# Expert counts read twelve at a time, and the scatter planes paired, read back in 2 KB pieces and transposed later

## The chip, the cores and the metric

The kernel runs on one core of one Trainium2 chip. The metric is the device time of one execution in microseconds (us): the median of several runs.

## What is computed

The reference is a two-layer backbone over 256 context and 256 latent tokens of width 1024. Layer 0 mixes by gated linear attention beside grouped-query attention, layer 1 by a state-space scan beside a Fourier mixing. Every layer ends in a mixture of experts, which is where the change lies. Cut to that part:

```
idx, gates = route(tokens, router_w, router_b)      # top 2 of 16 experts for each token
y = moe_ffn(tokens, idx, gates, w_gate, w_up, w_down)   # sum over a token's two experts of
                                                    # gate * (silu(t @ w_gate) * (t @ w_up)) @ w_down
x = layer_norm(alpha * x + m_lat[5] * y[...])       # and the same for the context in layer 0
```

There are 16 experts with an inner width of 768. Layer 0 routes 512 tokens (context and latent), layer 1 routes the 256 latent ones.

## The kernel before, in words

**The expert loop.** `experts` (L1474) runs once for each layer. It walks over 16 experts `e`, two of which form a pair `p`. The tokens of a pair are packed into two slot blocks S = 0 and S = 1 of 64 slots for each expert; parts of 32 tokens that hold nobody are skipped at run time. For each expert `hidden` (L1654) multiplies the packed tokens by the gate and up weights and applies SwiGLU, and `down` (L1696) multiplies by the down weights one expert later. The weights of an expert are six transfers of 1.5 MB each (four for gate and up, two for down, L1646 to L1650), issued in a fixed order by SyncE (SP, `wload`, L334) into a ring of slots; a transfer waits until TensorE has finished with its slot.

**Counts.** `counts` (L1404) writes a table `cnt` of 25 integers: the tokens of each of 16 experts, the larger count of each of 8 pairs, and the largest of all. TensorE's sequencer reads one of them whenever `count` (L1736) is called: once for each expert, and twice for each pair but the first (once as `full`, once for `features`). Each read is a `value_load` with bounds, that is a register load, a register operation and an assertion. The branches of `when` (L1483, L1487) compare these registers with constants. The reads depend on nothing but the table, so the scheduler may issue them long before their use, and in bundles. GpSimd (POOL) reads pair counts of its own for `gather` (L1557) and `scatter` (L1602).

**Two ways back to the tokens.** In layer 0 the outputs of the first six pairs (NS = 6) go through DRAM. `scatter` (L1595) sends each pair's rows by indirect DMA into four DRAM tiles `plane0` to `plane3`, one for each quarter of 256 columns; a token has two rows there, one for each of its two experts. When pair 5 is scattered (at e = 12), `fetch(0)` (L1607) reads the 256 context tokens back with 16 DMAs of 128 KB on POOL's queue and adds the two rows on POOL; `collect` (L1619) transposes the sums on TensorE and adds them into the residual on VectorE (L1592). `collect(got, 0)` stands at the end of e = 13, where `fetch(1)` follows it into the same buffer, and `collect(got, 1)` at the end of e = 14. The remaining pairs, and all pairs of layer 1, go back by `combine` (L1629): VectorE builds eight one-hot matrices (L1588), in a buffer that shares its tag `rb` (one buffer) with that of `fetch`, and TensorE multiplies by them. `combine` of pair 6 runs in `between` (L1773) of e = 15.

**Order.** TensorE's matmuls in the loop are pinned to the order of the text (`self.pin`, L1760), except inside the branches of `when`. `between` runs after the first two parts of an expert's gate and up products, `middle` inside them. POOL's queue carries the scatters, the gathers of the next pairs' tokens (L1561) and the fetches, each in one order.

```
L1737  return nc.tensor.value_load(cnt[0:1, i:i + 1], min_val=0, max_val=T)
L1613  nc.gpsimd.dma_start(rb[:, j, i, q * 256:(q + 1) * 256], self.planes[q][o:o + 128])
L1801  if ns and 1 <= e - 2 * ns <= 2:
L1802      collect(got, e - 2 * ns - 1)
L1803      if e == 2 * ns + 1:
L1804          got = fetch(1)
```

## Time and profile before

| what | value |
|---|---|
| runs of the kernel before, us | 1477.24, 1477.56, 1483.76 (median 1477.56) |
| the profiled execution's own time, us | 1479.13 |
| its span in the profile, us | 1477.4 |
| mean granted TensorE clock, share of full speed | 0.921 |
| TensorE matmul busy (PE) | 1250.3 us, 85% |
| TensorE weight load (PEld) | 726.9 us, 49% |
| VectorE (DVE) | 682.2 us, 46% |
| ScalarE (ACT) | 398.0 us, 27% |
| GpSimd (POOL) | 140.8 us, 10% |
| transfers on SP's queue (q1) | 388.40 MB, 64.6% of 16 engines' span |
| transfers on POOL's queue (q0) | 17.71 MB, 3.3% |

The span is one execution from its first to its last instruction; the profiled execution's own time is a little longer than its span. Times in the rows are microseconds from the span's start, unless they are means or medians of one instruction, which are nanoseconds where the view says so. A timeline's row gives start, length, engine, line and operation, and in brackets how long the engine had been idle and what ended that; "issue" there means that the profile shows nothing it waited for. The letter q behind an engine (PEldq, SPq) stands for its sequencer.

### The profile page before, as it was taken

The numbers are of one execution on the slowest core, as the hardware profiler recorded it, in microseconds if no ns is written. First come the engines' busy times: TensorE is split into PE (matmuls) and PEld (weight loads), VectorE is DVE, ScalarE is ACT, GpSimd is POOL, SyncE is SP. The second block draws the span as 40 slices with busy tenths as digits, with TensorE's granted clock in tenths as the row PEclk, the third lists the DMA queues.
The fourth block names the chain that finished last, engine by engine and source line by source line (L and its number), as shares of the span: only waits on it lengthen the run. The fifth ranks groups of instructions, "written<-read, shape, count | busy, mean of one in ns | idle before, by whom it ended". The sixth has DMA issues, their size and how long they took to land. (4 is left out here: it accounts for less than half of the span.)

```text
span 1477.4 us, 27647 instructions
## 1 busy us (share of the span) xinstructions
PE 1250.3 (85%) x11433; PEld 726.9 (49%) x11434; DVE 682.2 (46%) x1773; ACT 398.0 (27%) x791; POOL 140.8 (10%) x153
## 2 busy tenths in 40 slices
PE   4999988898679799999878867998978688898774
PEld 0697553576334344554434435876833344454333
DVE  1847536876425111111123568737665245454445
ACT  2624234344110110111010134434431112121214
POOL 0000011102101111022133012002010000000000
PEclk8999999899799999999989988999989898998996
DMA  9421688134488998889998341273388999999981
GB/s 359 163 100 43 223 323 343 52 128 161 178 338 315 382 412 369 347 329 421 426 386 341 144 160 55 89 278 150 129 340 360 377 412 425 423 426 421 425 367 31
DMA packets 49475, 411.87 MB, mean 279 GB/s; under 512 B 7195, under 2 KB 11439, under 8 KB 18064
## 3 DMA queue, kind: packets, MB, share of 16 engines
q1 hardware_dynamic: 41200, 388.40, 64.6%
q0 software_dynamic: 7232, 17.71, 3.3%
q8 instruction: 140, 2.29, 0.6%
q10 hardware_dynamic: 864, 3.15, 0.5%
q14 instruction: 39, 0.32, 0.1%
HBM read 402.02 MB, written 13.11 MB: 281 GB/s over the span
## 5 line engine op out<-in xcount | busy, mean ns | idle before, releaser
L1665 DVE SCALAR_TENSOR_TENSOR h0p<-gu0p,gt0p,sg0p 128x192 f32<-128x192 f32 x64 | 25.3, 415 | 177.0 <-ACT sg0p L321 176.5
L345 PE MATMUL gu0p<-big,xe0p 128*32 128x384 f32 x992 | 91.8, 492 | 1.6 <-issue 1.4
L345 PE MATMUL gu1p<-more,big 128*32 128x384 f32 x976 | 85.5, 493 | 7.9 <-issue 3.0
L321 ACT ACTIVATE sg0p<-gu0p 128x192 f32<-128x192 f32 x64 | 19.6, 331 | 247.1 <-PE gu0p L345 243.8
L345 PE MATMUL gu0p<-ring,xe0p 128*32 128x384 f32 x768 | 74.8, 497 | 0.8 <-ACT sg0p L321 0.5
L345 PE MATMUL gu0p<-more,xe0p 128*32 128x384 f32 x800 | 74.7, 493 | 0.5 <-issue 0.5
L345 PE MATMUL ada<-ring,small 128*32 128x512 f32 x344 | 62.9, 684 | 14.2 <-DMA ring<-in_ada 14.2
L1665 DVE SCALAR_TENSOR_TENSOR h1p<-gu1p,gt1p,sg1p 128x192 f32<-128x192 f32 x48 | 19.9, 415 | 118.0 <-ACT sg1p L321 117.9
L345 PE MATMUL dp0p<-big,hT0p 128*32 128x256 f32 x792 | 59.4, 402 | 6.3 <-issue 4.0
L345 PEld LDWEIGHTS gu1p<-more,big 128*32 128x32 f32 x976 | 35.1, 111 | 51.3 <-issue 46.1
L345 PEld LDWEIGHTS gu0p<-big,xe0p 128*32 128x32 f32 x992 | 37.8, 111 | 45.4 <-issue 42.1
L321 ACT ACTIVATE y0p<-dp0p 64x512 f32<-64x512 f32 (+1 forms) x40 | 23.6, 591 | 132.9 <-PE dp0p L345 105.0
L321 ACT ACTIVATE y1p<-dp1p 64x512 fp32r<-64x512 f32 x64 | 37.9, 592 | 79.9 <-PE dp1p L345 79.1
L321 ACT ACTIVATE sg1p<-gu1p 128x192 f32<-128x192 f32 x48 | 15.9, 330 | 156.4 <-PE gu1p L345 141.0
L321 ACT ACTIVATE big<-big 128x512 f32<-128x512 f32 (+2 forms) x81 | 44.7, 575 | 48.8 <-DVE big L641 21.5
L1598 POOL DMA_INDIRECT plane<-y0p,to0p x36 | 35.6, 988 | 205.8 <-ACT y0p L321 180.0
L345 PE MATMUL zo<-zo,zw 128*128 128x256 f32 x384 | 54.7, 292 | 0.0
L345 PE MATMUL gu1p<-big 128*32 128x384 f32 x528 | 52.5, 510 | 0.0
L345 PE MATMUL dp0p<-ring,hT0p 128*32 128x256 f32 x624 | 48.9, 401 | 3.5 <-issue 3.2
L345 PEld LDWEIGHTS zo<-zo,zw 128*128 128x128 f32 x384 | 48.6, 191 | 6.6 <-issue 4.3
L345 PEld LDWEIGHTS <-zero 128*128 128x128 bf16 x105 | 10.0, 97 | 83.2 <-issue 64.8
L1730 DVE TENSOR_TENSOR y1p<-dp1p,y1p 64x512 fp32r<-64x512 f32 x64 | 44.0, 688 | 5.5 <-ACT y1p L321 3.9
(558 smaller groups left out, 2425.2 us busy)
## 6 DMA issues: line engine op xcount, KB each, us to landing
more<-in_egu SPq DMA_DIRECT2D x54, 1536.0 KB, 15.3
big<-in_egu SPq DMA_DIRECT2D x48, 1536.0 KB, 15.6
ring<-in_ada SPq DMA_DIRECT2D x27, 1536.0 KB, 8.0
ring<-in_ed SPq DMA_DIRECT2D x27, 1536.0 KB, 14.8
ring<-in_egu SPq DMA_DIRECT2D x26, 1536.0 KB, 13.5
big<-in_ed SPq DMA_DIRECT2D x21, 1536.0 KB, 12.9
more<-in_ed SPq DMA_DIRECT2D x16, 1536.0 KB, 10.7
ring<-in_odw SPq DMA_DIRECT2D x5, 1536.0 KB, 6.2
```

Of the source, the lines that this page charges most:

```text
L321: a = self.nc.scalar.activation(out, x, func, **kw)
L345: i = self.nc.tensor.matmul(out, lhsT, rhs, start=start, stop=stop, skip_group_check=True)
L1598: nc.gpsimd.indirect_dma_start(out=self.planes[q], out_offset=bass.IndirectOffsetOnAxis(ap=to[:, q, i, S:S + 1], axis=0), in_=Y[S][:, q // ...
L1665: nc.vector.scalar_tensor_tensor(H[:, t], p[:, 192:384], gt[:, 2 * m + t % 2, i, t // 2:t // 2 + 1], sg, op0=OP.mult, op1=OP.mult)
L1730: nc.vector.tensor_tensor(yl[r, q], dp[r], yh[r, q].bitcast(F32), op=OP.subtract)
```

## The change

Four things are changed, all in the expert stage.

1. The table of counts has the order first expert, second expert, larger of both, for each pair. TensorE reads it with one call for 12 entries (8 experts, 4 pairs) without assertions: at the start of the loop, and again at e = 6, queued behind the last matmul traced so far. `count` only looks the value up.
2. The four planes of 256 columns become two DRAM tiles, each with two quarters side by side (quarter `q` of a row is piece `2 * row + q % 2` of plane `q // 2`). The scatter's row numbers are doubled accordingly, and its four DMAs go out in the order 0, 2, 1, 3.
3. `fetch` reads with four DMAs of 512 KB, in pieces of 2 KB, instead of 16.
4. `collect(got, 1)` moves from the end of e = 14 to `between` of e = 15, ahead of `combine` of pair 6.

```
--- before.py
+++ after.py
@@ -343,6 +343,7 @@
 
     def mm(self, out, lhsT, rhs, start=True, stop=True):
         i = self.nc.tensor.matmul(out, lhsT, rhs, start=start, stop=stop, skip_group_check=True)
+        self.last = i.ins
         if self.pin:
             self.tc.keep_in_program_order(i)
 
@@ -450,11 +451,11 @@
 
     def open_planes(self, pool):
         nc = self.nc
-        z = pool.tile([128, 256], F32, name='zeros')
+        z = pool.tile([128, 512], F32, name='zeros')
         nc.gpsimd.memset(z, 0.0)
-        self.planes = [self.dram.tile([2 * T, 256], F32, name=f'plane{q}') for q in range(4)]
+        self.planes = [self.dram.tile([4 * T, 256], F32, name=f'plane{q}') for q in range(2)]
         for p in self.planes:
-            nc.gpsimd.dma_start(p.rearrange('(a p) d -> p a d', p=128), z.unsqueeze(1).broadcast_to([128, 8, 256]))
+            nc.gpsimd.dma_start(p.rearrange('(a p c) d -> p a (c d)', p=128, c=2), z.unsqueeze(1).broadcast_to([128, 8, 512]))
 
     def layer0(self):
         nc, tc = self.nc, self.tc
@@ -1404,17 +1405,18 @@
     def counts(self, l, count):
         nc, pm, rp = self.nc, self.pm, self.rp
         NP = NE // 2
-        cf = rp.tile([128, NE + NP + 1], F32, tag='r_cf', name=f'cf{l}')
-        nc.vector.tensor_copy(cf[:, :NE], count)
-        nc.vector.tensor_reduce(cf[:, NE:NE + NP], cf[:, :NE].rearrange('p (q m) -> p q m', m=2), axis=AX.X, op=OP.max)
-        nc.vector.tensor_reduce(cf[:, NE + NP:], cf[:, :NE], axis=AX.X, op=OP.max)
-        cnt = pm.tile([128, NE + NP + 1], I32, tag='r_cnt', name=f'cnt{l}')
+        cf = rp.tile([128, 3 * NP + 1], F32, tag='r_cf', name=f'cf{l}')
+        c3 = cf[:, :3 * NP].rearrange('p (q x) -> p q x', x=3)
+        nc.vector.tensor_copy(c3[:, :, 0:2], count.rearrange('p (q m) -> p q m', m=2))
+        nc.vector.tensor_reduce(c3[:, :, 2], c3[:, :, 0:2], axis=AX.X, op=OP.max)
+        nc.vector.tensor_reduce(cf[:, 3 * NP:], c3[:, :, 2], axis=AX.X, op=OP.max)
+        cnt = pm.tile([128, 3 * NP + 1], I32, tag='r_cnt', name=f'cnt{l}')
         nc.vector.tensor_copy(cnt, cf)
 
         wf = rp.tile([128, 2, NP], F32, tag='r_wf', name=f'wf{l}')
-        nc.vector.tensor_scalar(wf[:, 0], cf[:, NE:NE + NP], 0.0, None, op0=OP.is_gt)
+        nc.vector.tensor_scalar(wf[:, 0], c3[:, :, 2], 0.0, None, op0=OP.is_gt)
         for w in range(WIN[l], T >> l, WIN[l]):
-            nc.vector.tensor_scalar(wf[:, 1], cf[:, NE:NE + NP], float(w), None, op0=OP.is_gt)
+            nc.vector.tensor_scalar(wf[:, 1], c3[:, :, 2], float(w), None, op0=OP.is_gt)
             nc.vector.tensor_tensor(wf[:, 0], wf[:, 0], wf[:, 1], op=OP.add)
         nwin = pm.tile([128, NP, 2], I32, tag='r_nw', name=f'nwin{l}')
         nc.vector.tensor_copy(nwin, wf[:, 0].unsqueeze(2).broadcast_to([128, NP, 2]))
@@ -1483,13 +1485,13 @@
         def when(rv, least, yes, no=None):
             if rv is None:
                 return yes()
-            pin, self.pin = self.pin, False
+            pin, self.pin, last = self.pin, False, self.last
             with tc.If(rv > least) as cmp:
                 yes()
             if no:
                 with cmp.Else():
                     no()
-            self.pin = pin
+            self.pin, self.last = pin, last
 
 
 
@@ -1548,13 +1550,13 @@
                     if tail:
                         nc.vector.tensor_copy(tok[r, q], tg[s, 0, n - tail:])
                     if n > tail:
-                        nc.vector.tensor_copy(to[r, q], tg[s, 2])
+                        nc.vector.tensor_scalar(to[r, q], tg[s, 2], 2.0, q % 2 * 1.0, op0=OP.mult, op1=OP.add)
                     nc.vector.tensor_copy(gt[r, c ^ q], tg[s, 1])
             return idx, tok, gt, to
 
         def gather(idx, i, S, e=None):
             if S and e is not None:
-                n = nc.gpsimd.value_load(cnt[0:1, e:e + 1], min_val=0, max_val=T)
+                n = nc.gpsimd.value_load(cnt[0:1, 3 * e + 2:3 * e + 3], min_val=0, max_val=T)
                 with tc.If(n > 64):
                     gather(idx, i, S)
                 return
@@ -1594,12 +1596,12 @@
 
         def scatter(Y, to, i, e):
             def send(S):
-                for q in range(4):
-                    nc.gpsimd.indirect_dma_start(out=self.planes[q], out_offset=bass.IndirectOffsetOnAxis(ap=to[:, q, i, S:S + 1], axis=0),
+                for q in (0, 2, 1, 3):
+                    nc.gpsimd.indirect_dma_start(out=self.planes[q // 2], out_offset=bass.IndirectOffsetOnAxis(ap=to[:, q, i, S:S + 1], axis=0),
                                                  in_=Y[S][:, q // 2, (q % 2) * 256:(q % 2) * 256 + 256].bitcast(F32), in_offset=None,
-                                                 bounds_check=2 * tn - 1, oob_is_err=False)
+                                                 bounds_check=4 * T - 1, oob_is_err=False)
             send(0)
-            n = nc.gpsimd.value_load(cnt[0:1, e:e + 1], min_val=0, max_val=T)
+            n = nc.gpsimd.value_load(cnt[0:1, 3 * e + 2:3 * e + 3], min_val=0, max_val=T)
             with tc.If(n > 64):
                 send(1)
 
@@ -1607,10 +1609,10 @@
         def fetch(a):
             rb = pm.tile([128, 2, 2, D], F32, tag='rb', name=f'rows{a}')
             for j in range(2):
-                for i in range(2):
-                    for q in range(4):
-                        o = i * T + a * TC + j * 128
-                        nc.gpsimd.dma_start(rb[:, j, i, q * 256:(q + 1) * 256], self.planes[q][o:o + 128])
+                for q in range(2):
+                    o = a * TC + j * 128
+                    nc.gpsimd.dma_start(rb[:, j, :, q * 512:q * 512 + 512],
+                                        self.planes[q].rearrange('(i t c) d -> t i (c d)', i=2, c=2)[o:o + 128])
             for j in range(2):
                 nc.gpsimd.tensor_tensor(rb[:, j, 0], rb[:, j, 0], rb[:, j, 1], op=OP.add)
             return rb[:, :, 0]
@@ -1733,8 +1735,17 @@
         def outputs(nm, n):
             return [[pm.tile([128, 2, 512], F32R, tag=f'y{S}', bufs=2, name=f'y{l}{nm}{S}{h}') for h in range(n)] for S in range(2)]
 
+
+        def some_counts(e):
+            i = 3 * (e // 2)
+            _, n = nc.values_load_multi_w_load_instructions(cnt[0:1, i:i + 3 * NC // 2], engines=[mybir.EngineType.PE], min_val=0, max_val=T,
+                                                                skip_runtime_bounds_check_because='counts of T tokens, compared with constants only')
+            for p in range(NC // 2):
+                ns_[e + 2 * p], ns_[e + 2 * p + 1], ns_[NE + e // 2 + p] = n[3 * p:3 * p + 3]
+
         def count(i):
-            return nc.tensor.value_load(cnt[0:1, i:i + 1], min_val=0, max_val=T)
+            return ns_[i]
+        ns_, NC = {}, 8
         info = {}
         ns = 0 if l else NS
 
@@ -1746,20 +1757,24 @@
 
         def gathers(p):
             for S in range(2):
-                gather(info[p][0][0], info[p][1], S, NE + p)
+                gather(info[p][0][0], info[p][1], S, p)
         xe, G0 = [], []
         idx = some_lists(0, 1, lambda G: features('p0', None, xe, (0,), G))
         if l == 0:
             self.gate = gather(idx, 0, 0).ins
         cnt, nwin = self.counts(l, number)
+        some_counts(0)
         if l == 0:
             with tc.issue_after(self.gate):
-                gather(idx, 0, 1, NE)
+                gather(idx, 0, 1, 0)
 
         nxt, last, Y, pend = xe if l else features('p0', None, xe, (0,)), None, None, None
         self.pin = True
         for e in range(NE):
             p, m = divmod(e, 2)
+            if e == NC - 2:
+                with tc.issue_after(self.last):
+                    some_counts(NC)
             if m == 0:
                 xe, ((idx, tok, gt, to), i) = nxt, info[p]
                 ti = i - (NS - 2 if i else 0)
@@ -1775,6 +1790,8 @@
                     features('p0', full, xe, (1,), G0)
                     some_lists(1, 1)
                     gathers(1)
+                if ns and e == 2 * ns + 3:
+                    collect(got, 1)
                 if m == 1 and pend:
                     combine(*pend)
 
@@ -1798,11 +1815,10 @@
                     scatter([y[0] for y in Y], *was[3:])
                     if p == ns:
                         got = fetch(0)
-            if ns and 1 <= e - 2 * ns <= 2:
-                collect(got, e - 2 * ns - 1)
-                if e == 2 * ns + 1:
-                    got = fetch(1)
-            last, was = [f'p{p}{m}', m, (f'p{p}{m}', H), rv], (tok, ti, full, to, i, NE + p)
+            if ns and e == 2 * ns + 1:
+                collect(got, 0)
+                got = fetch(1)
+            last, was = [f'p{p}{m}', m, (f'p{p}{m}', H), rv], (tok, ti, full, to, i, p)
             if e == 1 and l == 0:
                 some_lists(2, NP - 2)
         down(*last[:2], transposed(*last[2]), load_d(NE - 1), rv, Y)
@@ -1813,7 +1829,7 @@
             self.ada(1, 1, 'pj', pm.tile([128, 1024], F32, tag='xe0', name='adarow')[:, :512])
             self.pin = pin
 
-        most = nc.values_load(cnt[0:1, NE + NP:NE + NP + 1], min_val=0, max_val=T)
+        most = nc.values_load(cnt[0:1, 3 * NP:3 * NP + 1], min_val=0, max_val=T)
         with tc.If(most > WIN[l]):
             pw = pm.tile([128, nb, 2], F32, name=f'pw{l}')
             aw = pm.tile([128, nb, 2, NAUX[l]], F32 if l else F32R, name=f'aw{l}')
```

## Rows read from the trace of the kernel before

**Rows 1.** Stretches: start:end, length, busy (instructions) by engine, clock, DMA share, GB/s.

```profile
580.00:660.00 80.00, 77.70 (x1076) 40.40 (x1069) 9.47 (x18) 9.92 (x24) 10.89 (x11) 1.00 0.80 325
660.00:804.00 144.00, 120.10 (x1424) 58.93 (x1420) 30.80 (x57) 19.43 (x44) 39.42 (x49) 0.92 0.99 404
...
1172.00:1180.00 8.00, 6.55 (x61) 4.56 (x53) 3.23 (x9) 1.74 (x5) 0.00 (x0) 1.00 0.52 197
1180.00:1437.00 257.00, 215.77 (x2413) 106.85 (x2412) 117.42 (x401) 53.43 (x107) 5.94 (x6) 0.91 1.00 419
```

**Rows 2.** The counts' reads on TensorE's sequencer (L1737), whole span: ns minimum/median/maximum.

```profile
L1737 PEldq TENSOR_LOAD <-cnt x62: 295/300/488, 382.7 to 1164.8; - x62
L1737 PEldq FUSED_REGOPS  x62: 146/146/160, 383.3 to 1165.2; - x62
```

**Rows 3.** The same line in the stretches 484 to 512 and 1140 to 1153.

```profile
L1737 PEldq TENSOR_LOAD <-cnt x15: 297/300/319, 485.0 to 507.8; - x15
...
L1737 PEldq TENSOR_LOAD <-cnt x17: 295/300/312, 1140.9 to 1152.0; - x17
```

**Rows 4.** TensorE's waits, 380 to 855: us in total, times, longest.

```profile
PE xt0p L350 <- DMA xg<-rows,idx0p: 6.0, 1, 6.0
```

**Rows 5.** Timeline of TensorE, layer 0, 484 to 512.

```profile
486.77 0.59 PE L345 MATMUL xt0p<-zero 128*128 128x512 bf16 x2 [1.46 <-ACT sg0p L321]
...
501.65 2.79 PE L345 MATMUL gu0p<-more,xe0p 128*32 128x384 f32 x32 [0.47 <-issue]
505.08 2.79 PE L345 MATMUL gu0p<-big,xe0p 128*32 128x384 f32 x32 [0.64 <-issue]
508.77 0.34 PE L345 MATMUL gu0p<-zero 128*128 128x384 bf16 x1 [0.90 <-issue]
```

**Rows 6.** Timeline of TensorE, layer 1, 1140 to 1165.

```profile
1153.10 2.79 PE L345 MATMUL dp1p<-big,hT1p 128*32 128x256 f32 x24 [9.51 <-issue]
...
1164.76 9.24 PE L345 MATMUL gu1p<-more,big 128*32 128x384 f32 x112 [2.75 <-issue]
```

**Rows 7.** Timeline of SP's queue: start, time over which it issued, transfers.

```profile
751.90 0.33 SPq L338 DMA_DIRECT2D ring<-in_ed  x1
...
1160.34 0.33 SPq L338 DMA_DIRECT2D big<-in_ed  x1
...
1176.16 1.87 SPq L338 DMA_DIRECT2D more<-in_egu  x4
```

**Rows 8.** Timeline of POOL, the last scatter and fetch(0).

```profile
733.84 0.98 POOL L1598 DMA_INDIRECT plane<-y0p,to0p  x1 [32.02 <-ACT y0p L321]
...
744.22 0.62 POOL L1613 DMA_DIRECT2D rows<-plane  x1 [5.55 <-DMA plane<-y0p,to0p]
...
750.46 4.22 POOL L1613 DMA_DIRECT2D rows<-plane  x8 [0.95 <-DMA rows<-plane]
...
766.62 2.34 POOL L1615 TENSOR_TENSOR rows<-rows 128x1024 f32<-128x1024 f32 x1 [9.54 <-issue]
```

**Rows 9.** Scatters' DMAs (L1598): from issue to landing.

```profile
DMA to landing us min/median/max: 2.3/7.4/8.6
```

**Rows 10.** POOL's DMA queue, 755 to 767: packets, MB, share of 16 engines.

```profile
q0 software_dynamic: 241, 0.66, 14.0%
```

**Rows 11.** POOL: a gather behind the first pair's scatters; TensorE: its first use.

```profile
492.84 1.05 POOL L1561 DMA_INDIRECT xg<-rows,idx0p  x1 [2.51 <-DMA plane<-y0p,to0p]
...
522.72 0.55 PE L350 MATMUL xt0p<-const,xg 128*128 128x128 f32 x3
```

**Rows 12.** Timeline of TensorE at collect(0) and collect(1).

```profile
769.01 2.61 PE L350 MATMUL cl<-const,rows 128*128 128x128 f32 x11 [8.21 <-POOL rows L1615]
771.55 2.53 PE L345 MATMUL gu0p<-more,xe0p 128*32 128x384 f32 x14
...
798.90 3.46 PE L350 MATMUL cl<-const,rows 128*128 128x128 f32 x15 [4.76 <-POOL rows L1615]
```

**Rows 13.** VectorE's one-hot matrices of layer 0 (L1588): ns minimum/median/maximum.

```profile
L1588 DVE TENSOR_SCALAR oh0p<-const,tok0p x16: 445/478/486, 804.5 to 833.6; 128x512 fp32r<-128x512 f32 x16
```

More of the change, by code (lines that the diff above doesn't have):

```diff
@@ L452, in open_planes @@
         nc = self.nc
-        z = pool.tile([128, 256], F32, name='zeros')
+        z = pool.tile([128, 512], F32, name='zeros')
         nc.gpsimd.memset(z, 0.0)
-        self.planes = [self.dram.tile([2 * T, 256], F32, name=f'plane{q}') for q in range(4)]
+        self.planes = [self.dram.tile([4 * T, 256], F32, name=f'plane{q}') for q in range(2)]
         for p in self.planes:
-            nc.gpsimd.dma_start(p.rearrange('(a p) d -> p a d', p=128), z.unsqueeze(1).broadcast_to([128, 8, 256]))
+            nc.gpsimd.dma_start(p.rearrange('(a p c) d -> p a (c d)', p=128, c=2), z.unsqueeze(1).broadcast_to([128, 8, 512]))
     def layer0(self):
@@ L1491, in when @@
                     no()
-            self.pin = pin
+            self.pin, self.last = pin, last
         def entries(p, i, S, G, aux):
@@ L1734, in outputs, with some_counts @@
             return [[pm.tile([128, 2, 512], F32R, tag=f'y{S}', bufs=2, name=f'y{l}{nm}{S}{h}') for h in range(n)] for S in range(2)]
+        def some_counts(e):
+            i = 3 * (e // 2)
+            _, n = nc.values_load_multi_w_load_instructions(cnt[0:1, i:i + 3 * NC // 2], engines=[mybir.EngineType.PE], min_val=0, max_val=T,
+                                                                skip_runtime_bounds_check_because='counts of T tokens, compared with constants only')
+            for p in range(NC // 2):
+                ns_[e + 2 * p], ns_[e + 2 * p + 1], ns_[NE + e // 2 + p] = n[3 * p:3 * p + 3]
         def count(i):
-            return nc.tensor.value_load(cnt[0:1, i:i + 1], min_val=0, max_val=T)
+            return ns_[i]
+        ns_, NC = {}, 8
         info = {}
@@ L1762, in experts @@
             p, m = divmod(e, 2)
+            if e == NC - 2:
+                with tc.issue_after(self.last):
+                    some_counts(NC)
             if m == 0:
@@ L1777, in between @@
                     gathers(1)
+                if ns and e == 2 * ns + 3:
+                    collect(got, 1)
                 if m == 1 and pend:
@@ L1800, in experts @@
                         got = fetch(0)
-            if ns and 1 <= e - 2 * ns <= 2:
-                collect(got, e - 2 * ns - 1)
-                if e == 2 * ns + 1:
-                    got = fetch(1)
-            last, was = [f'p{p}{m}', m, (f'p{p}{m}', H), rv], (tok, ti, full, to, i, NE + p)
+            if ns and e == 2 * ns + 1:
+                collect(got, 0)
+                got = fetch(1)
+            last, was = [f'p{p}{m}', m, (f'p{p}{m}', H), rv], (tok, ti, full, to, i, p)
             if e == 1 and l == 0:
```

45 lines of the change are left out of this document (24 added, 21 removed).

## The prediction, made before the changed kernel ran

> **What bounds the kernel now.** The stretches come first. In layer 0 the weights' transfers and TensorE take turns: DMA is busy 0.80 from 580 to 660, where TensorE works 77.70 of 80 us, and 0.99 from 660 to 804. In layer 1 the stream of weights is the bound: DMA 1.00 from 1180 to 1437, after a dip to 0.52 from 1172 to 1180 [rows 1]. So a microsecond saved on TensorE in layer 0 counts while weights wait for slots to come free, and in layer 1 only as far as it closes a gap in the stream. The waits, the timelines of TensorE, POOL and SP, and the counts' reads were read next, for what holds TensorE up and would change.
>
> *The counts.* TensorE's sequencer makes 62 reads; a register load takes 0.30 us (0.49 at most) and its bounds operation 0.15 [rows 2]. 17 of them start between 1140.9 and 1152.0 [rows 3], so one read with assertion and issue takes 11.1 / 16 = 0.69 us. In layer 1 the 17 stand in one bundle ahead of a down product, which starts after 9.51 us of idle time; some of the rest cost 2.75 us in the next product [rows 6]. In layer 0, 15 reads lie between 485.0 and 507.8 [rows 3], and the idle times there are 1.46, 0.47, 0.64 and 0.90 us [rows 5]: between bundles TensorE still has queued matmuls.
>
> *The fetches.* TensorE stands 8.21 us before the transposes of collect(0) and 4.76 before those of collect(1), both times for POOL's sums [rows 12]. Back from there on POOL: the second half of fetch(0), eight DMAs, is issued from 750.46 to 754.68, and its sum starts only at 766.62; the fetch itself began at 744.22, when the scatters of 733.84 had landed [rows 8]. From 751.90 on SP issues weights beside it [rows 7], and POOL's queue then moves 0.66 MB in 12 us, 55 GB/s [rows 10].
>
> **Part 1, reads.** Four calls take the place of 62. None of the rows shows a load of twelve. Below, it costs 0.30, like a load of one register; above, twelve loads without the assertion: 0.69 less the operation's 0.15 and some 0.15 of assertion and issue leave about 0.40 each, 4.8 us a call. I take 0.5, by the slowest single load (0.49) [rows 2], because it is one call on one range. The first call of layer 0 lies in the 6.0 us for which TensorE waits for the gather [rows 4], and so did the first reads before: nothing (if that gather came sooner, 0.5). In layer 0 the idle times add up to 1.46 + 0.47 + 0.64 + 0.90 = 3.5; less 0.5 for the call at e = 6: **-3.0**.
>
> In layer 1 TensorE gets 9.51 + 2.75 = 12.3 us ahead, but its weights don't. What it frees earlier: the down weights of 1160.34 and the gate and up weights of 1176.16 are asked for up to 12 us sooner [rows 7], and that fills the dip between 1172 and 1180: 8 x (1 - 0.52) = 3.8 us [rows 1]. After it the stream is full and only moves forward. The call at e = 6 hides behind queued transfers. **-3.8** (-3 to -5, as TensorE may keep a little more of its lead at the end). What is late next: the weights themselves.
>
> The Trainium skill ("Runtime: NRT & Kernel Launch", Instruction fetch mechanics) speaks against the cheap call: register loads cost about 200 ns for each register even in bulk, an estimated 2.4 us for twelve; the sum would be about 2 us smaller for the call in mid layer 0. The trace shows loads of one register alone.
>
> **Part 2, planes and scatter.** Doubling the row numbers turns a copy into a multiply-add of the same tiny shape: nothing, as VectorE is not late there. Two tiles instead of four make each second scatter wait for the one before it on the same tile; the order 0, 2, 1, 3 puts one other scatter between. A landing takes 7.4 us [rows 9] and an issue 0.98 [rows 8], about 1.3 with the step to the next, so the four scatters of a slot block go out at 0, 1.3, 7.4 and 8.7 instead of within 4, and the eight of a pair with slots in S = 1 take about 24 us instead of 13. Behind the waiting scatter on POOL stand the gathers of a later pair. The tightest is the one at 492.84, used at 522.72 [rows 11]: it goes out up to 11 us later, at 504, and even if it needs twice a scatter's 7.4 us it has landed by 519: nothing; if that cover is gone, the wait at these transposes is a few us. Before collect(0) nothing covers it: the scatters of 733.84 now go out at 733.8, 735.1, 741.2 and 742.5 and land near 749 and 750, where the fetch started at 744.22 before [rows 8].
>
> **Part 3, fetch.** Four DMAs of 512 KB for sixteen of 128 KB. An issue took 4.22 / 8 = 0.53 [rows 8]; with twice the pieces I take 0.5 to 1.1 each. The last goes out near 752.5 instead of 754.2, although the first is 5 us later. What flows before the weights of 751.90 bite is fast; what is left crawls: at 55 GB/s, or up to twice that if a piece of 2 KB takes its turn like one of 1 KB. The second half then lands between 757 and 769; I take 762, its sum (2.34) ends at 764.4 and TensorE goes on at 764.8 where it did at 769.01. Its idle time began at 760.8, so 4 us of 8.21 are left: -4.2. After the old wait 14 matmuls took 2.53 us, 0.18 each, at 0.09 for the same shape elsewhere (2.79 / 32) [rows 5, 12], half the pace, as at the lower of the two clock levels; with half the wait I count 0.8 of these 1.3: **-5.0** in all (bounds: -9.5, no wait, to +1, a wait as long and an issue more).
>
> **Part 4, collect(1) moved.** Its 4.76 us wait goes: fetch(1) starts after collect(0) and has until e = 15. The transposes are only moved. But the one-hot matrices of pair 6 share the buffer, and they had been made while TensorE did gate and up; now they can start only after the last transpose, behind the last adds on VectorE, and TensorE's combine stands behind them. The first matrix costs 0.48, all eight 3.8 [rows 13]; the matmuls need one for each four of theirs, so I take 2.0 with the adds: **-2.8** (-4.3 to -1.0).
>
> Zeroing two larger planes instead of four early in layer 0 is off every path: nothing.
>
> **Sum.** -3.0 - 3.8 - 5.0 - 2.8 = -14.6 us. The profiled execution took 1479.13 (span 1477.4), which would give 1464.5; it stands 1.57 above the median of the runs, 1477.56. Against the median: 1463.0, 1.0% less. A measurement of this kernel can tell about 0.5% (7.4 us) from no change.
>
> **Rivals.** *The pieces don't matter* (chance 0.15). POOL's queue gets its turns in units that don't depend on the piece, so it stays at 55 GB/s beside the weights. For it: the low rate with sixteen DMAs in hand [rows 10]; against: each DMA less saves its own ending. Of the 2.1 MB I estimate 0.6 left at 754.5; they take 11 us, to 765.5; the wait is 7.2 and part 3 brings -1.0: 1467.0. The Trainium skill ("DMA: Bandwidth & Descriptors", SWDGE vs HWDGE vs iDMA) has such a rule: a queue keeps its turn for a packet of up to about 4096 bytes, not for one piece. No row here gives the pieces of a packet.
>
> *One register at a time* (0.12). The call does not do what it says: twelve loads, 4.8 us. Layer 0's reads then bring +1.3 instead of -3.0, and the start of layer 1's experts stands 4.8 us less two old reads' 1.4, so 3.4 later. For it: nothing in the trace has read two values at once; against: one call. 1477.56 + 1.3 + 3.4 - 3.8 - 5.0 - 2.8 = 1470.7.
>
> *The stream takes it back* (0.12). TensorE, ahead in layer 0, finds its weights not landed, and only layer 1's dip closes: 1473.8. For it: DMA at 0.99 from 660 to 804; against: 0.80 from 580 to 660, and no wait for expert weights among TensorE's.
>
> *The fetch falls into the weights* (0.09, ends slower). The two waits on a plane push the whole fetch past 751.90. That decides: if the last landing comes after it, 2.1 MB share the engines with the weights until these are through, near 780. The sum ends at 782.5, a wait of 21.7 for 8.21, +13.5: 1477.56 - 3.0 - 3.8 - 2.8 + 13.5 = 1481.5. For it: my margin is 2 us; against: the fetch's first half moves freely if it starts near 749.
>
> **How the numbers follow.** The forecast has 0.52, at 1463. The range 1454 to 1475 takes in the bounds of its parts (all at their best about -22, 1455, and a little of what the lead in layer 1 may add), the first three rivals and leaves out the fourth. Over 0.5% faster means below 1470.2: 0.50 of the forecast, 0.12 of the first rival, 0.06 of the second, 0.01 of the third, 0.69. Slower by over 0.5%: 0.06 of the last rival, where the stall costs a little more than I counted. The rest, 0.25, is no change.
>
> **What would show it.** Right: four register loads on TensorE's sequencer in place of the 62; no idle time of 9.51 in layer 1 and no dip of DMA near 1172; scatters of one pair in twos, about 7 us apart; four fetch DMAs ending near 752, a wait at collect(0) of about 4 us and none at collect(1), but about 2 before the combine of pair 6. Wrong: loads in groups of twelve, fetch landings as late as 766, or TensorE waiting for expert weights in layer 0. A new order of TensorE's or POOL's queue from the scheduler would make all of it wrong.

## The result, and the profile after

The change makes the kernel slower, where the forecast was 1.0% faster.

| | median of 13 runs, us | lowest to highest |
|---|---|---|
| before | 1479.97 | 1475.01 to 1483.81 |
| after | 1491.78 | 1485.28 to 1501.99 |

The ratio is 1.0088, with a 95% interval from 1.0068 to 1.0107: 12 to 13 us lost. The profiled execution of the changed kernel took 1494.68 us (span 1492.9).

**What came as forecast.** The reads are four calls. These are the rows of the changed kernel that answer to [rows 2] (TensorE's sequencer, nanoseconds minimum/median/maximum), then to [rows 6] (timeline of TensorE in layer 1, the down product and the gate and up products behind it) and to the last but one of [rows 1] (the stretch 1172 to 1180, which lies between e = 2 and e = 3 of layer 1 here).

```profile
L1741 PEldq TENSOR_LOAD <-cnt x4: 850/860/1058, 394.6 to 1241.6; - x4
```

```profile
1164.97 1.55 PE L345 MATMUL dp1p<-big,hT1p 128*32 128x256 f32 x23
...
1171.25 10.53 PE L345 MATMUL gu1p<-more,big 128*32 128x384 f32 x128 [0.30 <-PEq L1489]
```

```profile
1172.00:1180.00 8.00, 8.00 (x108) 3.87 (x103) 2.64 (x4) 1.06 (x2) 0.00 (x0) 1.00 1.02 431
```

The 9.51 and 2.75 us are gone, and so is the dip in the stream of weights. Yet the span is 15.6 us longer. To find where the time went, set the two executions side by side by the start of each expert's first SwiGLU product on VectorE: the changed kernel is 1.4 us late at e = 1 of layer 0 and 24.5 late at e = 2.

**The first loss.** Timeline of VectorE, the first SwiGLU product of e = 2: before, then after.

```profile
461.40 0.42 DVE L1665 SCALAR_TENSOR_TENSOR h0p<-gu0p,gt0p,sg0p 128x192 f32<-128x192 f32 x1 [1.11 <-ACT sg0p L321]
```

```profile
485.91 0.42 DVE L1667 SCALAR_TENSOR_TENSOR h0p<-gu0p,gt0p,sg0p 128x192 f32<-128x192 f32 x1 [4.64 <-ACT sg0p L321]
```

Now TensorE ahead of it, before: `sl0p` are products of `lists` for pairs 2 to 7 (four matmuls for each one-hot matrix `G0p` that VectorE makes), `dp0p` the down products of e = 1, `gu0p` gate and up of e = 2.

```profile
447.82 0.61 PE L345 MATMUL sl0p<-aux,G0p 128*128 128x10 f32 x4
448.36 2.46 PE L345 MATMUL gu0p<-ring,xe0p 128*32 128x384 f32 x27
...
451.08 0.61 PE L345 MATMUL sl0p<-aux,G0p 128*128 128x10 f32 x4
451.62 1.50 PE L345 MATMUL gu0p<-more,xe0p 128*32 128x384 f32 x16
```

After:

```profile
448.88 0.61 PE L345 MATMUL sl0p<-aux,G0p 128*128 128x10 f32 x4
450.07 1.46 PE L345 MATMUL dp0p<-big,hT0p 128*32 128x256 f32 x18 [0.58 <-ACT y0p L321]
...
471.06 1.01 PE L345 MATMUL sl0p<-aux,G0p 128*128 128x10 f32 x4 [0.79 <-DVE G0p L1515]
472.86 1.01 PE L345 MATMUL sl0p<-aux,G0p 128*128 128x10 f32 x4 [0.79 <-DVE G0p L1515]
473.81 5.22 PE L345 MATMUL gu0p<-ring,xe0p 128*32 128x384 f32 x32
```

Before, gate and up of e = 2 fill the time in which VectorE makes the next matrix. After, all twelve of these groups come first and gate and up start 25 us later, at 473.81. TensorE's order has changed. What it costs shows in the stretch 446 to 474 (columns as in [rows 1]), before and after:

```profile
446.00:474.00 28.00, 27.75 (x327) 13.89 (x323) 14.60 (x50) 2.98 (x7) 2.24 (x3) 1.00 0.86 350
```

```profile
446.00:474.00 28.00, 24.73 (x182) 14.58 (x178) 10.77 (x16) 1.77 (x3) 4.10 (x4) 0.62 0.33 128
```

TensorE gets through 182 matmuls instead of 327. It waits for VectorE again and again, its granted clock is 0.62 on average for 1.00 (four `sl0p` matmuls take 0.61 us early in the stretch and 1.01 late in it), and as no weight slot comes free, the transfers stand: 0.33 for 0.86. At these shares 28 x (0.86 - 0.33) = 15 us of a full stream of weights aren't moved. They don't come back as a wait: no idle time of TensorE from e = 0 to 5 is put down to a weight transfer. What the order costs TensorE itself stands below, at `before_chained`.

**The second loss** is the fetch. The rows of after that answer to [rows 8], [rows 7] and [rows 12]: POOL's timeline, SP's, TensorE's.

```profile
751.57 1.00 POOL L1600 DMA_INDIRECT plane<-y0p,to0p  x1 [22.64 <-ACT y0p L321]
752.88 0.99 POOL L1600 DMA_INDIRECT plane<-y0p,to0p  x1 [0.30 <-issue]
758.79 0.98 POOL L1600 DMA_INDIRECT plane<-y0p,to0p  x1 [4.92 <-DMA plane<-y0p,to0p]
760.36 0.98 POOL L1600 DMA_INDIRECT plane<-y0p,to0p  x1 [0.59 <-DMA plane<-y0p,to0p]
767.36 2.99 POOL L1614 DMA_DIRECT2D rows<-plane  x4 [6.03 <-DMA plane<-y0p,to0p]
...
789.59 2.34 POOL L1617 TENSOR_TENSOR rows<-rows 128x1024 f32<-128x1024 f32 x1 [7.73 <-DMA rows<-plane]
```

```profile
768.11 0.33 SPq L338 DMA_DIRECT2D ring<-in_ed  x1
```

```profile
781.91 0.47 PE L351 MATMUL cl<-const,rows 128*128 128x128 f32 x1 [5.08 <-POOL rows L1617]
791.98 2.61 PE L351 MATMUL cl<-const,rows 128*128 128x128 f32 x11 [9.60 <-POOL rows L1617]
...
832.50 1.84 PE L345 MATMUL cm0p<-oh0p,y0p 128*128 128x512 f32 x6 [2.24 <-DVE oh0p L1590]
```

The scatters go out in twos, and the fetch starts 15.8 us after the first of them (10.4 before), 0.75 us ahead of the next weights. The second sum ends at 791.9. collect(0) waits 5.08 + 9.60 = 14.7 us where it waited 8.21. The wait of collect(1) is gone, with 2.24 us in its place.

### The profile page after: what moved, and what is told of

Its sections match the earlier page's. It is cut to its first block, busy times and chain, and to the rows that moved or that the text cites. A ratio compares the mean times of both kernels' runs of the same rounds, so it can differ in the third digit from the quotient of the medians.

```text
span 1492.9 us, 27409 instructions
## 1 busy us (share of the span) xinstructions
PE 1256.3 (84%) x11433; PEld 753.1 (50%) x11434; DVE 682.8 (46%) x1773; ACT 398.6 (27%) x791; POOL 128.1 (9%) x127
## 5 line engine op out<-in xcount | busy, mean ns | idle before, releaser
L345 PE MATMUL gu1p<-more,big 128*32 128x384 f32 x976 | 85.5, 494 | 12.3 <-DMA more<-in_egu 6.1
L321 ACT ACTIVATE sg0p<-gu0p 128x192 f32<-128x192 f32 x64 | 19.5, 329 | 237.6 <-PE gu0p L345 217.6
L345 PE MATMUL dp0p<-big,hT0p 128*32 128x256 f32 x792 | 64.4, 420 | 11.3 <-issue 8.7
L345 PEld LDWEIGHTS gu0p<-big,xe0p 128*32 128x32 f32 x992 | 43.5, 110 | 36.7 <-issue 27.6
L1600 POOL DMA_INDIRECT plane<-y0p,to0p x36 | 35.7, 992 | 266.5 <-ACT y0p L321 217.6
L345 PE MATMUL dp0p<-ring,hT0p 128*32 128x256 f32 x624 | 52.5, 417 | 0.3 <-PEq L1489 0.2
L345 PEld LDWEIGHTS gu0p<-more,xe0p 128*32 128x32 f32 x800 | 32.7, 112 | 36.9 <-issue 28.1
L345 PEld LDWEIGHTS gu0p<-ring,xe0p 128*32 128x32 f32 x768 | 34.0, 113 | 33.4 <-issue 24.0
## 6 DMA issues: line engine op xcount, KB each, us to landing
ring<-in_egu SPq DMA_DIRECT2D x26, 1536.0 KB, 15.8
```

Source lines behind the costliest of these rows:

```text
L321: a = self.nc.scalar.activation(out, x, func, **kw)
L345: i = self.nc.tensor.matmul(out, lhsT, rhs, start=start, stop=stop, skip_group_check=True)
L1600: nc.gpsimd.indirect_dma_start(out=self.planes[q // 2], out_offset=bass.IndirectOffsetOnAxis(ap=to[:, q, i, S:S + 1], axis=0), in_=Y[S][:, ...
```

## The experiments

Theory A for the first loss: `keep_in_program_order` ties a matmul to the instruction traced just before it on TensorE. Where a read stood, that was the read's own instruction, which nothing ties, so the chain was open there, and the scheduler, which sets the order of each engine's queue, could move the next expert's products up. With 58 of the 62 loads gone, the chain closes at these places. Theory E for the second: the fetch starts late and falls among the weights. The kernels, each against the kernel before on the same chip:

| kernel | median, us | ratio to before [95%] |
|---|---|---|
| after | 1491.78 | 1.0088 [1.0068, 1.0107] |
| `after_freed` | 1476.00 | 0.9980 [0.9961, 0.9998] |
| `after_free_one` | 1480.89 | 1.0002 [0.9980, 1.0024] |
| `before_chained` | 1488.44 | 1.0051 [1.0031, 1.0071] |
| `counts_only` | 1491.06 | 1.0083 [1.0057, 1.0109] |
| `planes_only` | 1484.00 | 1.0018 [1.0006, 1.0031] |
| `counts_freed` | 1480.61 | 1.0021 [1.0002, 1.0041] |
| `freed_late` | 1472.52 | 0.9973 [0.9956, 0.9990] |
| `freed_late8` | 1465.22 | 0.9914 [0.9892, 0.9936] |
| `freed_16` | 1482.82 | 1.0032 [1.0012, 1.0052] |
| `before_late8` | 1472.88 | 0.9940 [0.9916, 0.9963] |
| `freed_hold` | 1469.94 | 0.9929 [0.9907, 0.9952] |

The kernel before had a median of 1478.94 beside `after_freed`, `before_chained`, `counts_only` and `planes_only`, 1477.29 beside `counts_freed` to `freed_16`, and 1482.77 beside `after_free_one`, `before_late8` and `freed_hold`. So ratios are compared, not medians.

**`after_freed`: the chain opened where the reads stood.**

```
 def mm(...):
-    if self.pin:
-        self.tc.keep_in_program_order(i)
+    self.pinned(i)
...
+def pinned(self, i):
+    if self.pin and not self.free:
+        self.tc.keep_in_program_order(i)
+    self.free = self.free and not self.pin
...
 def count(i):
+    self.free = self.pin
     return ns_[i]
```

> The changed kernel, in which the first TensorE instruction traced after a place where a count used to be read is not held in program order; nothing else differs. Theory A (order: each old read broke the chain that holds TensorE's instructions in program order, and without it gate and up of expert 2 wait behind all twelve list products): the lists of pairs 2 to 6 stand among these products again, expert 2 starts some 20 us sooner than in the changed kernel, the 12 us lost in layer 0 come back and the lead in layer 1 shows: 1470 us, between 1465 and 1477, 0.98 to 0.99 of the changed kernel. Rival B (planes and fetch cost the time): the order is no matter, 1488 to 1494. Rival C (the calls of twelve cost it): 1488 to 1494 too.

Measured: 0.9980, so 1.1% below the changed kernel, some 16 us. No instruction is added or taken away; only ties are. In 446 to 474 TensorE is as before:

```profile
446.00:474.00 28.00, 27.88 (x327) 13.84 (x319) 13.67 (x43) 2.40 (x6) 0.99 (x1) 0.99 0.88 358
```

What follows: the order alone turns a small gain into the loss. B and C fall for this loss.

**`before_chained`: the reverse, reads kept and the chain closed.**

```
+        old = (j for j in reversed(self.nc.cur_bb.bb.instructions) if j is not i.ins and j.engine == i.ins.engine)
+        prev = next((j for j in old if j.name not in self.reads), None)
+        if prev is not None:
+            self.tc.add_manual_dep(i.ins, prev.name, NOSYNC)
```

> The kernel before with its 62 reads, its four planes and its sixteen fetches, in which a read no longer breaks the chain of program order: a TensorE instruction is held behind the last one on its engine that is not a read. Theory A: the list products of pairs 2 to 6 all come ahead of gate and up of expert 2, as in the changed kernel; expert 2 starts 15 to 25 us later, 12 of it last, and since the reads still cost what they did: 1488 to 1500 us, 1.007 to 1.015 of the kernel before. Rivals B and C: no change, 1478 within 4.

Measured: 1.0051. A had the sign, but its range (from 1.007) was missed. TensorE's timeline and the stretch show the order of the changed kernel, with gate and up of e = 2 at 469.07 and four planes and 62 reads as before:

```profile
468.13 1.01 PE L345 MATMUL sl0p<-aux,G0p 128*128 128x10 f32 x4 [0.79 <-DVE G0p L1518]
469.07 4.64 PE L345 MATMUL gu0p<-ring,xe0p 128*32 128x384 f32 x32
```

```profile
446.00:474.00 28.00, 22.43 (x221) 13.00 (x217) 15.21 (x55) 1.78 (x3) 8.83 (x9) 0.82 0.36 136
```

So the loss can be had without any part of the change. It is half as large here, and the traces say where. From e = 0 to 5 TensorE's idle time (gaps over 50 ns) is 17.7 us in the changed kernel and 11.7 in `after_freed`, 22.9 here and 18.5 in the kernel before: the order costs 6.0 and 4.4. The rest of the stretch, in which TensorE works, grows by 8.6 us there (110.2 for 101.6) and by 1.6 here (103.7 for 102.1). The granted clock from 446 to 474 is 0.62 there and 0.82 here. So most of the difference is what TensorE lost by the lower clock; why it fell further there stays open.

**`counts_only` and `planes_only`: the parts alone.** The diffs are those of the change, part 1 in the one, parts 2 to 4 in the other.

> The kernel before with the new table and the four calls of twelve alone; planes, scatters, fetch and collect as before. Theory A: all of the loss but the fetch's share, so 1483 to 1492 us although 58 loads are gone; expert 2 of layer 0 starts some 20 us late, expert 3 of layer 1 gains 10 to 14 us on expert 2. Rival B (the planes cost it): the reads' 7 us are gained, 1468 to 1473. Rival C (the calls cost it): 1488 to 1494 with the loss at the calls.

> The kernel before with two planes, scatters in the order 0, 2, 1, 3, four fetches of 512 KB and the transposes of the second half later; the 62 reads as before. Theory A: TensorE's order at expert 2 is that of before; collect(0) waits about 14 us instead of 8, the wait of collect(1) of about 5 is gone, some 2 us stand before the combine of pair 6: 1476 to 1484 us. Rival B (the planes cost it): 1488 to 1494. Rival C: 1470 to 1478.

Measured: 1.0083 and 1.0018, both as A had it. Part 1 carries nearly the whole loss though it takes 58 loads away. In `counts_only` e = 2 is 21.1 us late in layer 0, and its step from e = 2 to e = 3 in layer 1 takes 16.8 us for 30.4: the gain is there too. In `planes_only` the wait of collect(0) is 3.44 + 9.58 = 13.0:

```profile
771.73 0.48 PE L350 MATMUL cl<-const,rows 128*128 128x128 f32 x1 [3.44 <-POOL rows L1615]
781.79 2.61 PE L350 MATMUL cl<-const,rows 128*128 128x128 f32 x11 [9.58 <-POOL rows L1615]
```

That is as much as both waits of before together, 8.21 + 4.76 [rows 12].

**`after_free_one`: the ties of one pair undone.** The edit against `after_freed`. It opens the chain where the counts of expert 2 and of its pair were read: these are two places, ahead of the transposes of that pair's tokens at the end of e = 1 and ahead of the first product of e = 2, not one as the expectation says.

```
-    self.free = self.pin
+    self.free = self.pin and l == 0 and i in (2, NE + 1)
```

> The changed kernel with the chain of program order opened at one place alone: at the first TensorE instruction after the old reads of expert 2 in layer 0. Theory A (the order at expert 2 is most of the loss): the twelve list products stand among gate and up of expert 2, which starts 20 us sooner than in the changed kernel; of the 16 us between the changed kernel and after_freed 10 to 16 come back: 1476 to 1482 us. Rival H (all the breaks together do it, here and in layer 1): under 6 us come back, 1486 to 1492.

Measured: 1.0002, so 0.86 of the 1.08 points between the changed kernel and `after_freed` come back with these two places open. A holds; the 0.22 that are left are within the interval.

```profile
449.59 0.61 PE L345 MATMUL sl0p<-aux,G0p 128*128 128x10 f32 x4
450.12 2.46 PE L345 MATMUL gu0p<-ring,xe0p 128*32 128x384 f32 x27
```

**`counts_freed`: part 1 with the chain open.** The edit of `after_freed` on `counts_only`.

> The kernel before with the new table and the four calls of twelve alone, and the chain of program order open where the old reads stood. Theory A (order, and the reads are worth what they cost): TensorE's order at expert 2 is that of before; layer 0 gains 3 to 7 us between experts 0 and 5, layer 1 some 5; against counts_only 10 to 16 us less: 1470 us, between 1466 and 1474. Rival D (the weights take every lead back, in both layers): 1476 to 1480.

Measured: 1.0021. A's number was missed and D's was met in this kernel: 0.6 points below `counts_only`, and no faster than before. Its layer 1 is shorter (359.5 us from the first SwiGLU product to the end, 365.6 before), but in layer 0 the lead is lost again; the table below shows where. `after_freed` has parts 2 to 4 on top and is 0.4 points faster, though these parts cost 0.18 points by themselves (`planes_only`). No stretch of the table shows that gain, and the two ran on different chips: it stays open.

**`freed_late` and `freed_late8`: the fetch with four planes.** The first is `counts_freed` with collect(1) late; the second also reads both slots with one DMA.

```
-    for i in range(2):
-        for q in range(4):
-            o = i * T + a * TC + j * 128
-            nc.gpsimd.dma_start(rb[:, j, i, q * 256:(q + 1) * 256], self.planes[q][o:o + 128])
+    for q in range(4):
+        o = a * TC + j * 128
+        nc.gpsimd.dma_start(rb[:, j, :, q * 256:q * 256 + 256],
+                            self.planes[q].rearrange('(i t) d -> t i d', i=2)[o:o + 128])
```

> The kernel above with the transposes of the second half moved to expert 15 as in the change; four planes, scatters without a wait, sixteen fetches of 128 KB. Theory E (what is lost at the fetch is its start behind the two waits on a plane): the fetch starts some 10 us after the first scatter, collect(0) waits 8 us as before, the second wait of about 5 is gone, 2 us stand ahead of the combine of pair 6: 1467 us, between 1463 and 1472, 3 less than the kernel above. Rival D: the same as the kernel above within 2.

> The kernel above with eight fetches of 256 KB, both slots in one, still in pieces of 1 KB. Theory E and number of transfers without weight: as the kernel above within 2 us, collect(0) waits 7 to 9. Rival F (the number of DMAs sets the rate of the fetch, not the piece): the last half lands 3 to 6 us sooner, collect(0) waits 2 to 5.

Measured: 0.9973 and 0.9914. `freed_late` gains 0.5 points on `counts_freed`, more than expected, and collect(0) waits 9.2. `freed_late8` is the fastest kernel of the study, in pieces of 1 KB, and TensorE doesn't wait for the sums at all. POOL's timeline and SP's next weights:

```profile
741.37 0.98 POOL L1603 DMA_INDIRECT plane<-y0p,to0p  x1 [0.30 <-issue]
747.57 0.80 POOL L1617 DMA_DIRECT2D rows<-plane  x1 [5.22 <-DMA plane<-y0p,to0p]
749.04 5.07 POOL L1617 DMA_DIRECT2D rows<-plane  x7 [0.67 <-DMA plane<-y0p,to0p]
757.25 2.35 POOL L1620 TENSOR_TENSOR rows<-rows 128x1024 f32<-128x1024 f32 x1 [3.13 <-DMA rows<-plane]
760.13 2.37 POOL L1620 TENSOR_TENSOR rows<-rows 128x1024 f32<-128x1024 f32 x1 [0.54 <-DMA rows<-plane]
```

```profile
755.52 0.33 SPq L338 DMA_DIRECT2D ring<-in_ed  x1
```

Eight issues take 0.72 us each, sixteen took 0.53 [rows 8]. All eight are out at 754.1, 1.4 us ahead of the weights of 755.52; in the kernel before the issue of the sixteenth ended 2.8 us behind them. The time from the first fetch to these weights is the same (7.95 us here, 7.68 before), so it is the issue that is faster: 256 KB in 0.72 us are 364 GB/s, 128 KB in 0.53 are 247. Rival F had the sign, and more than the size: the number of DMAs decides how much is issued before the weights are, and `freed_16` shows that it sets the rate beside them too.

**`freed_16`: sixteen DMAs again.** `after_freed` with 16 DMAs in pieces of 1 KB from the two planes; the number of DMAs and the piece change together.

> after_freed with sixteen fetches in pieces of 1 KB from the two planes; scatters in twos with their waits as in the change. Theory E and pieces of 2 KB that do help: the fetch starts as late as in after_freed and needs longer, the sum of the second half ends 4 to 12 us later than there, collect waits 18 to 25 in all where after_freed has 14: 1480 to 1487 us. Rival G (the pieces don't matter beside the weights): 14 us as there, 1474 to 1478.

Measured: 1.0032, as E had it; collect waits 9.66 + 11.48 = 21.1 us.

```profile
775.30 0.48 PE L350 MATMUL cl<-const,rows 128*128 128x128 f32 x1 [9.66 <-POOL rows L1621]
787.26 2.61 PE L350 MATMUL cl<-const,rows 128*128 128x128 f32 x11 [11.48 <-POOL rows L1621]
```

The sizes of all packets, and POOL's DMA queue beside the weights (packets, MB, share of 16 engines), first `after_freed` from 756 to 773, then `freed_16` from 763 to 784:

```profile
DMA packets 943, 6.99 MB, mean 411 GB/s; under 512 B 111, under 2 KB 111, under 8 KB 506
...
q0 software_dynamic: 459, 1.62, 25.7%
```

```profile
DMA packets 1227, 8.64 MB, mean 412 GB/s; under 512 B 268, under 2 KB 268, under 8 KB 652
...
q0 software_dynamic: 575, 1.57, 19.1%
```

1.62 MB in 17 us are 95 GB/s, 1.57 in 21 are 75: a factor of about 1.3. E's number was met, but the piece isn't the reason. Read packet by packet, POOL's queue has only two sizes in both kernels: 4096 bytes, whatever the piece, and 4 bytes, 16 of these for each DMA. Beside the weights it gets through the same number of packets, 459 / 17 = 27.0 per us and 575 / 21 = 27.4. With sixteen DMAs a third of them are the small ones (191 of 575), with four a seventh (64 of 459). So the number of DMAs makes the factor, and the premise of rival G holds though its time doesn't. No run changes the piece and keeps the number of DMAs.

**`freed_hold`: the weights held back.** `after_freed`, in which the next weights wait for the fetch.

```
     d = self.nc.sync.dma_start(t[:, :n], src)
+    if self.behind:
+        self.tc.add_manual_dep(d.ins, self.behind.name, SYNC)
...
+    self.behind = first if ns and e == 2 * ns + 2 else None
     Wd = load_d(e - 1) if e else None
+    self.behind = None
```

> after_freed, in which the two down-weight transfers that SP issues while the first fetch is on its way wait for the last of the four fetches (and what is queued behind them on SP with them). Theory E: the 2.1 MB then land within 10 us of the first issue instead of 20, collect(0) waits 2 to 6 us where it waited 14, and the weights held back some 8 us are not missed: 1464 to 1470 us. Rival G (the four DMAs are slow by themselves): collect(0) still waits 10 or more, and the weights come later on top: 1478 to 1486.

Measured: 0.9929, 0.5 points below `after_freed`, with the same four fetches behind the same waits on a plane. POOL, SP, TensorE, and POOL's queue from 756 to 764:

```profile
755.03 3.00 POOL L1620 DMA_DIRECT2D rows<-plane  x4 [6.24 <-DMA plane<-y0p,to0p]
761.37 2.38 POOL L1623 TENSOR_TENSOR rows<-rows 128x1024 f32<-128x1024 f32 x1 [3.33 <-DMA rows<-plane]
764.78 2.35 POOL L1623 TENSOR_TENSOR rows<-rows 128x1024 f32<-128x1024 f32 x1 [1.03 <-DMA rows<-plane]
```

```profile
764.70 0.33 SPq L339 DMA_DIRECT2D ring<-in_ed  x1
```

```profile
767.18 2.61 PE L353 MATMUL cl<-const,rows 128*128 128x128 f32 x11 [2.04 <-POOL rows L1623]
```

```profile
q0 software_dynamic: 576, 2.10, 73.6%
```

Alone, the 2.1 MB take 8 us, 260 GB/s, at 72 packets per us. collect(0) waits 2.04 us for 14, and the weights that come 10 us later are not missed: TensorE has no wait for a weight transfer from 760 to 860. The loss at the fetch is the company it has, not its four DMAs by themselves: E holds, G falls.

**`before_late8`: what the reads are worth.** The kernel before with the eight fetches and collect(1) late.

> The kernel before with its 62 reads, with eight fetches of 256 KB and the transposes of the second half at expert 15; four planes as before. Theory E (all fetches must be out before the next weights are): the last fetch is issued before the weights that follow, collect(0) waits under 3 us where it waited 8, the second wait of about 5 is gone, 2 us stand ahead of the combine of pair 6: 1466 to 1471 us. If the calls of twelve are worth as much beside it as the trace of counts_freed has them (some 6 us in layer 1), it ends 2 to 6 us behind freed_late8 (1465.2); rival D (the weights take it back): level with it within 2, or ahead.

Measured: 0.9940, 0.26 points behind `freed_late8`. The last of the eight fetches is issued by 757.1, 0.9 us ahead of the next weights, and collect(0) doesn't wait: E holds with the reads too. The intervals of the two kernels overlap, and they ran on different chips; if it is real, the calls of twelve with the right order are worth some 4 us, where the forecast had 6.8.

## Why the prediction was wrong, step by step

This table is worked out from the starts of each expert's first SwiGLU product on VectorE, one profiled execution each, in us. Layer 0: from e = 0 to 5, 5 to 13, 13 to 15; layer 1: from e = 0 to the end of the span. The rows are read for single stretches and not summed, for two reasons. Where collect(1) is late, it and its wait fall behind the third stretch. And the time from e = 15 to layer 1, which isn't in the table, was 298.8 us in the profiled execution of before and 302.9 to 306.8 in all others, 303.2 in `before_chained`, which has the same work there. So 8 of the 15.6 us between the profiled executions of before and after lie in a stretch that this account doesn't explain.

| kernel | 0 to 5 | 5 to 13 | 13 to 15 | layer 1 |
|---|---|---|---|---|
| before | 120.6 | 210.2 | 69.2 | 365.6 |
| after | 127.9 | 217.5 | 66.1 | 359.9 |
| `after_freed` | 113.3 | 215.7 | 65.4 | 360.1 |
| `after_free_one` | 111.2 | 217.5 | 67.5 | 360.1 |
| `before_chained` | 126.6 | 212.1 | 64.9 | 367.3 |
| `counts_only` | 120.9 | 217.6 | 65.2 | 360.2 |
| `planes_only` | 123.1 | 212.4 | 69.3 | 363.4 |
| `counts_freed` | 112.1 | 216.5 | 64.3 | 359.5 |
| `freed_late8` | 111.6 | 216.9 | 50.7 | 360.0 |
| `freed_hold` | 112.9 | 219.9 | 52.6 | 359.7 |

**The step that failed: part 1's "what it removes".** The prediction priced the reads as time on TensorE's sequencer and let everything else stand where it was. It named "a new order of TensorE's or POOL's queue from the scheduler" as what would make all of it wrong, but gave it no mechanism and no chance. That was it: opening the chain again takes the changed kernel from 1.0088 to 0.9980, 16 us, more than the whole sum of -14.6. The trace of before had the clue. Its matmuls were called pinned to the order of the text, yet gate and up of e = 2 stand among the down products of e = 1 there. An order that the text doesn't give has to come from somewhere, and each read was such a place.

POOL's queue got a new order as well. POOL reads pair counts of its own, and ahead of the first gather stand four of these reads in the four kernels that keep TensorE's reads, and eight in all nine that don't. The gather goes out 2.5 us later (9.6 us behind the product `pos` for 7.1), and TensorE waits 8.8 us for it instead of the 6.0 of [rows 4]:

```profile
392.35 1.94 PE L351 MATMUL xt0p<-const,xg 128*128 128x128 f32 x8 [8.81 <-DMA xg<-rows,idx0p]
```

The prediction took this wait as given; it had only looked at what would follow if the gather came sooner.

**The reads' own price was right enough.** A call took 0.85 to 1.06 us for the 0.5 I took, the first of them 1.06. The Trainium skill's 200 ns for each register ("Runtime: NRT & Kernel Launch", Instruction fetch mechanics), an estimated 2.4 us for twelve, is not what the trace shows: 0.86 / 12 is 72 ns. The page gives its figure for loads that the runtime adds, not for reads of a table on the chip.

**-3.8 in layer 1 was right, if a little small.** Layer 1 is 5.4 to 6.1 us shorter in all kernels with the four calls, a little more than the part's range of 3 to 5. As the prediction had it, TensorE is 13 to 14 us ahead at e = 3 and the weights take most of it back: from 1420 to 1450 TensorE of the changed kernel waits for them.

```profile
PE gu1p L345 <- DMA more<-in_egu: 6.1, 3, 2.1
PE dp1p L345 <- DMA big<-in_ed: 1.9, 1, 1.9
```

**-3.0 in layer 0 came, and went again.** With the order of before, e = 0 to 5 takes 7 to 9 us less than before, more than the 3.0 forecast. Then 5 to 13 takes 5 to 10 more in every kernel without the 62 reads, and 1 to 2 more in the other three that have them. TensorE's idle time there (gaps over 50 ns) is 17 to 21 us in the nine kernels without, and 13 to 16 in the four with them. One stall stands out. The rows are of the changed kernel: branches on TensorE's sequencer from 546 to 556, and the product behind the longest of them.

```profile
L1489 PEldq COMPARE_BRANCH  x3: 187/217/5770, 547.7 to 548.8; - x3
```

```profile
554.71 1.92 PE L345 MATMUL dp0p<-more,hT0p 128*32 128x256 f32 x14 [3.64 <-PEq L1489]
```

A stall of 2.8 to 3.9 us stands at this down product in all nine kernels with the calls of twelve; in the four that keep their reads, all unexplained idle time of TensorE from e = 5 to 9 adds up to 0.8 to 1.6. What such stalls wait for can be read from the packets in the traces. In the changed kernel a packet of 16 KB on the instruction queue (q8) has landed at 553.12, 1.6 us before this product starts. In the thirteen traces every idle time of TensorE over 0.7 us from e = 5 to 13 that the profile puts down to "issue" or to TensorE's sequencer (56 of them) ends 1.2 to 1.7 us after such a packet, and every branch of more than 2 us on TensorE's sequencer after 380 us (176) ends 1.3 to 1.5 us after one. So these stalls wait for code. The Trainium skill has this of branches (the same section of "Runtime: NRT & Kernel Launch"): a taken branch whose target isn't among the loaded pages waits for a fetch of its page. The traces agree. From e = 5 to 13 these stalls add up to 6.0 to 6.8 us in the four kernels with the reads and to 8.9 to 12.3 in the nine without, so 2 to 6 of the 5 to 10 us are more of them. The kernel before has branches as long, at other places (5.81 us at 435.4). The program is shorter by the reads, so every branch lies elsewhere in the code; that this decides which of them takes long was not tried.

The rival "the stream takes it back" isn't seen in layer 0: from e = 0 to 15 no idle time of TensorE is put down to a weight transfer in any trace. What makes up the rest of the 5 to 10 us stays open.

**Part 2 was right.** Scatters went out in twos, and the fetch started 15.8 us after the first (16 forecast).

**Part 3 failed in one term: "I take 762".** Forecast -5.0; collect(0) waits 6.5 us longer instead. The rate was right: 2.07 MB in 20 us beside the weights in the changed kernel (POOL's queue, 769 to 789), 104 GB/s, inside "55 or up to twice that".

```profile
q0 software_dynamic: 569, 2.07, 28.0%
```

What was wrong is "what flows before the weights bite is fast": with a start 0.75 us ahead of the weights nothing had flowed, so all 2.1 MB went at that rate and not about half. The rival "the fetch falls into the weights" (0.09) had the place and the margin of 2 us; its price, a wait of 21.7 us, was too high, as the DMAs keep some share beside the weights. The rival "the pieces don't matter" kept its premise and lost its conclusion: POOL's queue got 27 to 28 packets per us beside the weights whatever the piece, but fewer DMAs mean fewer packets of 4 bytes, and so more MB (`freed_16`). Its 55 GB/s was too low as well, since the window of [rows 10] goes on after the fetch is through: from 756 to 764 the queue moved 0.64 MB, 80 GB/s, in 226 packets, 28 per us. The Trainium skill's rule that was cited for it ("DMA: Bandwidth & Descriptors", SWDGE vs HWDGE vs iDMA: a turn for a packet of up to about 4096 bytes) agrees with the trace, where the packets with data are of 4096 bytes.

**Part 4 was right.** No wait at collect(1), and 2.24 us ahead of the combine for the 2.0 taken.

With both losses mended, as in `freed_hold`, the change is worth 0.7%, 10.5 us of the 14.6; with old planes, eight fetches and an open chain (`freed_late8`), 0.9%. The rival "one register at a time" fell with the calls of 0.86 us.

## What to carry to other kernels

An instruction that is taken away may have been where a chain of ordering ties was open: before pricing its time, compare the order in which each engine's instructions stand with the order of the text, and ask what holds it. A transfer that shares the engines with a full stream is priced by how much of it is issued before the stream's next request, and beside the stream by its number of packets: fewer DMAs gave more, not larger pieces. And an order that makes TensorE wait can cost its clock too: 6.0 us of idle time here, and 8.6 us more in which it worked.

## What was not expected of the hardware

One load of twelve registers took 0.85 to 1.06 us, where a load of one took 0.30: about 50 ns for each further register, (0.86 - 0.30) / 11. Branches on TensorE's sequencer take up to 6.7 us (in `planes_only`), and which of them take long changes from kernel to kernel. Those of more than 2 us end 1.3 to 1.5 us after a packet of 16 KB on the instruction queue. And POOL's queue got 27 to 28 packets per us beside a full stream of weights, of 4096 bytes or of 4, which are 75 to 104 GB/s by the number of DMAs; 2.1 MB in four DMAs got 260 GB/s alone.
